# Three products taken through a LayerNorm on the unnormalized residual, with weights split further ahead

## The chip, the cores and the metric

The program runs on one core of one Trainium2 chip. The metric is the device time of one execution in microseconds (us). The kernel before took 2340.74 us (median of three executions, 2340.49 to 2344.26).

## The reference, cut to what matters

The model is a two-layer encoder on 256 tokens of width 1024, in fp32. In each layer two sub-layers are wrapped by a LayerNorm:

```python
h = x * (1.0 + scale1) + shift1
aq, ak, ..., gl = split(h @ w_in[l])            # 70 column blocks of 128
...                                             # four mixers, gated merge -> mix
x = layer_norm(ALPHA * x + gate1 * mix, ln_g[l, 0], ln_b[l, 0])      # "ln1"
h2 = x * (1.0 + scale2) + shift2
q = h2 @ wq ; s = q . subkeys ; top 16 per half                      # p_wq: 16 column blocks
y = sum of expert rows of u_tab, v_tab                               # u: 128 blocks, v: 128 blocks
x = layer_norm(ALPHA * x + gate2 * y, ln_g[l, 1], ln_b[l, 1])        # "ln2"
```

`layer_norm` is `(x - mean) * rsqrt(var + eps) * g + b`, over the 1024 features of each token.

## The kernel before, in words

Features lie on the partitions: a residual `r` is 8 chunks of 128 features by 256 tokens. All weights are streamed from HBM once. A product is one job: 128 output features by 256 tokens, summed over the 8 input chunks. Fp32 accuracy is reached with three fp32r passes: weight `w` and input `x` are each split in a high and a low part, and `prod` issues wlo·xhi, whi·xlo and whi·xhi for each chunk, so 24 matmuls of 128x256 (L238 to L240). The weight arrives by SyncE's DMA queue as `raw` (512 KB), ScalarE makes `whi` (L230), VectorE `wlo` = raw - whi (L233). There are three such pairs of buffers, so a product's split waits until the product three before it is done.

The jobs of one layer are, in this order: 70 w_in products with the mixers beside them, 16 w_br products (merge into `gacc`, split into `h`), 8 w_out products (each makes one chunk of `r`, L832, and its square and sums for the norm), ln1, 16 p_wq products (each with four small `ssc` matmuls, L905, and a search of the 16 largest on VectorE, `topk`, L93), 128 u and 128 v products, ln2. In front of a norm the weights of the next three products are already split ("areas": raw in `raws`, split in `areas`). Four norms are run: ln1 and ln2 of layer 0, ln1 of layer 1, and the last one, which writes the output.

A norm (`norm`) runs as follows. TensorE sums r and r² with matmuls against a vector of ones (`lnst`, L348); it repeats a product with no use (`warm`, L332) while it would wait. VectorE computes mean and rsqrt with three Newton steps on 128x2 values (L352 to L359). TensorE spreads the two rows over the partitions (`lnb`, L325). VectorE multiplies and adds (L369) chunk by chunk. Then for each chunk `emit` lets ScalarE apply the affine map g·(1+scale), b·(1+scale)+shift (L386, `hf`) and make the high part (L230, `h`), VectorE the low part (L233). The three area products take the chunks as they come. ScalarE also rescales the residual for the next norm (L396) and stores it to HBM (`xd`).

The program's text gives only the dependences. A scheduler reorders each engine's queue, within an engine everything is issued in the order of that queue, and every wait is on another engine's or a DMA's semaphore. `behind` and `InOrder` pin a few orders.

## Time and profile before

| | |
|---|---|
| median of three executions | 2340.74 us (2340.49 to 2344.26) |
| the profiled execution | 2339.15 us, of which the span is 2337.3 us |
| mean granted TensorE clock | 0.994 of full speed |
| TensorE busy | 2285.6 us of 2337.3, 98% |
| VectorE, ScalarE, GpSimd busy | 77%, 60%, 10% |
| chain of work that ended last | TensorE 88%, VectorE 5%, DMA 3%, ScalarE 2% |

TensorE (PE) is the bound nearly everywhere. A busy TensorE can still do work of no use: the `warm` matmuls count as busy. A matmul of 128x256 shows 0.28 us, but the next starts 0.12 us later; so 24 of them are 2.88 us of the engine. VectorE (DVE) instructions of 128x256 show 0.41 to 0.47 us and start 0.34 to 0.39 us apart; ScalarE (ACT) ones with a scale show 0.59 us and start 0.5 us apart.

### The profile page before, as it was taken

How to read it: one execution, taken by the hardware profiler on the slowest of the kernel's cores; microseconds unless marked ns; L12 is line 12 of the kernel's file. 1: busy time of each engine (PE TensorE's matmuls, PEld its weight loads, DVE VectorE, ACT ScalarE, POOL GpSimd, SP SyncE). 2: the span in 40 equal slices, each digit the busy share in tenths (PEclk: the TensorE clock that was granted, in tenths of full speed). 3: DMA queues.
4: the chain of work that ended last, by engine and by line, in shares of the span. 5: the costliest groups of instructions: out<-in, count | busy, mean ns of one | idle time of the engine just before them, and what ended most of it. 6: DMA issues, size and time to landing. Idle time of an engine off the chain costs nothing.

```text
span 2337.3 us, 41336 instructions
## 1 busy us (share of the span) xinstructions
PE 2285.6 (98%) x14624; PEld 2022.1 (87%) x14624; DVE 1806.1 (77%) x3867; ACT 1414.0 (60%) x3069; POOL 240.9 (10%) x282
## 2 busy tenths in 40 slices
PE   5999999999999999999999999999999999999998
PEld 4999999888888888888899999998888888888887
DVE  6778798997889677777666676889888896665555
ACT  5666645677776654545456665457777766454544
POOL 0000000222222200000000000102222222000000
PEclk9999999999999999999999999999999999999999
DMA  9666664788888988888754455548888889766663
GB/s 352 207 215 208 208 215 146 200 219 206 205 207 205 233 269 277 274 292 288 239 182 141 150 172 155 198 154 213 226 205 206 205 213 240 234 211 194 195 211 109
DMA packets 165326, 495.49 MB, mean 212 GB/s; under 512 B 19584, under 2 KB 57216, under 8 KB 161920
## 3 DMA queue, kind: packets, MB, share of 16 engines
q1 hardware_dynamic: 127248, 453.51, 61.6%
q0 software_dynamic: 36864, 33.57, 9.5%
q10 hardware_dynamic: 1008, 5.77, 0.7%
q8 instruction: 116, 1.90, 0.3%
q14 instruction: 90, 0.74, 0.1%
HBM read 450.57 MB, written 5.24 MB: 195 GB/s over the span
## 4 chain that ended last, share of the span: by engine, by line
PE 88%; DVE 5%; DMA 3%; ACT 2%; issue 1%; SPq 0%; ACTq 0%; DVEq 0%
PE main L246 18%; PE vacc L1120 10%; PE vacc L1122 10%; PE vacc L1121 10%; PE main L247 9%; PE main L238 8%; PE main L239 7%; PE main L240 7%; DVE wlo L233 1%; PE gw L1020 1%; PE gw L1021 1%; DVE topk L93 1%; DMA raw<-in_w_in 1%; PE pt L530 1%; DMA ada<-in_w_ada 1%
## 5 line engine op out<-in xcount | busy, mean ns | idle before, releaser
L233 DVE TENSOR_TENSOR wlo<-raw,whi 128x1024 fp32r<-128x1024 f32 x723 | 880.7, 1219 | 362.9 <-ACT whi L230 353.6
L230 ACT ACTIVATE whi<-raw 128x1024 fp32r<-128x1024 f32 x720 | 763.4, 1060 | 551.8 <-PE vacc L1122 304.9
L246 PE MATMUL main<-h,whi 128*128 128x512 f32 x2048 | 731.3, 400 | 0.4 <-ACT whi L230 0.4
L247 PE MATMUL main<-h,wlo 128*128 128x256 f32 x2048 | 573.6, 280 | 1.7 <-DVE wlo L233 1.7
L246 PEld LDWEIGHTS main<-h,whi 128*128 128x128 f32 x2048 | 384.4, 188 | 85.0 <-ACT whi L230 0.7
L238 PE MATMUL main<-h,wlo 128*128 128x256 f32 x1408 | 410.0, 292 | 4.3 <-DVE wlo L233 3.0
L1120 PE MATMUL vacc<-whi,wv 128*128 128x512 f32 (+1 forms) x1030 | 400.0, 389 | 2.1 <-ACT u L1076 1.9
L1121 PE MATMUL vacc<-wlo,wv 128*128 128x512 f32 (+1 forms) x1030 | 399.7, 388 | 0.0
L240 PE MATMUL main<-h,whi 128*128 128x256 f32 x1408 | 399.6, 284 | 0.0
L1122 PE MATMUL vacc<-whi,wv 128*128 128x512 f32 (+1 forms) x1030 | 399.5, 388 | 0.0
L239 PE MATMUL main<-h,whi 128*128 128x256 f32 x1408 | 398.9, 284 | 0.0
L247 PEld LDWEIGHTS main<-h,wlo 128*128 128x128 f32 x2048 | 386.3, 189 | 3.4 <-DVE wlo L233 3.0
L1077 POOL DMA_DIRECT2D u<-more x256 | 220.4, 861 | 707.4 <-ACT u L93 414.9
L238 PEld LDWEIGHTS main<-h,wlo 128*128 128x128 f32 x1408 | 270.4, 192 | 9.6 <-DVE wlo L233 4.8
L239 PEld LDWEIGHTS main<-h,whi 128*128 128x128 f32 x1408 | 270.9, 193 | 0.5
L240 PEld LDWEIGHTS main<-h,whi 128*128 128x128 f32 x1408 | 270.6, 192 | 0.1
L1120 PEld LDWEIGHTS vacc<-whi,wv 128*128 128x128 f32 x1030 | 193.2, 188 | 43.0 <-ACT u L1076 2.8
L1121 PEld LDWEIGHTS vacc<-wlo,wv 128*128 128x128 f32 x1030 | 193.3, 188 | 40.0 <-DVE wlo L233 0.5
L1122 PEld LDWEIGHTS vacc<-whi,wv 128*128 128x128 f32 x1030 | 193.3, 188 | 39.9
L309 POOL TENSOR_TENSOR lnss<-lnss,sq 128x256 f32<-128x256 f32 x22 | 20.3, 922 | 1373.3 <-ACT sq L304 1372.7
L1002 DVE TENSOR_TENSOR ohe<-iota,ijg 128x1024 f16<-128x1024 f16 x128 | 87.4, 685 | 17.4 <-PE gw L1021 17.4
L1075 ACT ACTIVATE more<-main 128x256 f32<-128x256 f32 x256 | 96.3, 376 | 4.7 <-PE main L247 4.7
(244 smaller groups left out, 2847.2 us busy)
## 6 DMA issues: line engine op xcount, KB each, us to landing
raw<-in_p_u SPq DMA_DIRECT2D x256, 512.0 KB, 4.5
raw<-in_p_v SPq DMA_DIRECT2D x256, 512.0 KB, 3.8
raw<-in_w_in SPq DMA_DIRECT2D x134, 512.0 KB, 4.0
u<-more POOLq DMA_DIRECT2D x256, 128.0 KB, 5.2
adav<-in_w_ada SPq DMA_DIRECT2D x56, 512.0 KB, 5.5
raw<-in_w_br SPq DMA_DIRECT2D x32, 512.0 KB, 3.6
raw<-in_p_wq SPq DMA_DIRECT2D x26, 512.0 KB, 3.5
mixA<-in_w_ada SPq DMA_DIRECT2D x24, 512.0 KB, 4.7
```

The costliest lines, as they stand in the source:

```text
L230: return S.activation(hi, src, AF.Copy, scale=scale)
L233: return V.tensor_tensor(lo, src, hi.bitcast(F32), op=OP.subtract)
L238: PE.matmul(out, wlo(c), x(c)[:, 0], start=c == 0, stop=False)
L239: PE.matmul(out, whi(c), x(c)[:, 1], start=False, stop=False)
L240: PE.matmul(out, whi(c), x(c)[:, 0], start=False, stop=c == n - 1)
L246: PE.matmul(out, whi(c), x(c), start=c == 0, stop=c == n - 1, skip_group_check=True)
L247: PE.matmul(out[:, 0], wlo(c), x(c)[:, 0], start=False, stop=c == n - 1, skip_group_check=True)
L1075: S.activation(more, out[:, 1], AF.Copy)
L1077: nc.gpsimd.dma_start(u, more, accum_op=OP.add)
L1120: PE.matmul(o, wl[:, tt], hi, start=first, stop=False, skip_group_check=o0 > 0)
L1121: PE.matmul(o, wh[:, tt], lo, start=False, stop=False, skip_group_check=o0 > 0)
L1122: PE.matmul(o, wh[:, tt], hi, start=False, stop=last, skip_group_check=o0 > 0)
```

## The change

At three of the four norms (all but the last) the first three products ("heads") no longer wait for the normalized input. They take `xr` = g·(1+scale)·r, split in high and low, which `early_chunk` makes for each chunk as soon as its residual is there (ScalarE L296, VectorE L297), with two more columns that carry the affine terms (128x258 instead of 128x256). The result is copied out of PSUM (`ho`, ScalarE L403), and when mean and rsqrt are known, `head` normalizes it: one ScalarE instruction (`hu`, L358), a VectorE multiply (L359) and add (L360). The 13 remaining p_wq products, or 67 w_in products, still take the normalized `h`. The warm matmuls are left at the last norm only, without the 14 behind `lnb`.

At ln1 the raw area weights go to a free slice of `state["m"]`, and are allocated, loaded and split ahead of the first w_out product. The w_out jobs are marked `over`: weights are split so far ahead that the products 4, 5 and 6 of p_wq are split during w_out. At ln2 of layer 0 six w_in weights rather than three are loaded and split in the v phase (`NHEAD`), and the w_ada loads there are spread over 4.5 rather than 5 jobs each.

```diff
+    def new_early(x, sc, sh, g, b):
...
+        V.tensor_tensor(fold[:, 0, 0], g, opsc, op=OP.mult)
...
+        S.activation(x[:, :, 0, T:], ss, AF.Copy)
+        V.tensor_tensor(x[:, :, 1, T:], ss, x[:, :, 0, T:].bitcast(F32), op=OP.subtract)
+
+    def early_chunk(r, m):
+
+        x, sc = state["xr"][:, m], fold[:, 0, 0, m:m + 1]
+        S.activation(x[:, 0, :T], r, AF.Identity, scale=sc)
+        V.scalar_tensor_tensor(x[:, 1, :T], r, sc, x[:, 0, :T].bitcast(F32), op0=OP.mult, op1=OP.subtract)
...
+    def head(j, o, b):
+
+        u = wk.tile([128, T], F32, name="hu", tag="t1k", bufs=6)
+        S.activation(u, b[1], AF.Identity, scale=o[:, T:T + 1], bias=o[:, T + 1:])
+        V.tensor_tensor(o[:, :T], o[:, :T], b[0], op=OP.mult)
+        V.tensor_tensor(o[:, :T], o[:, :T], u, op=OP.add)
+        j.mm = lambda hi, lo: o[:, :T]
+
+    def norm(r, emit, heads=(), banks=()):
...
-        warm(early)
+        if not heads:
+            warm(6)
...
-        warm(22)
+        if not heads:
+            warm(22)
...
-        if state["ready"] is not state.get("last_hi"):
-            warm(14)
+        todo = []
+        for j, k in zip(heads, banks):
+            out = bank(k, [128, XW], name="head")
+            prod(out, lambda c: j.split[0][:, c], lambda c: j.split[1][:, c], lambda c: state["xr"][:, c], NC8)
+            o = wk.tile([128, XW], F32, name="ho", tag="more", bufs=4)
+            S.activation(o, out, AF.Copy)
+            todo.append(lambda j=j, o=o: head(j, o, b))
         for m0, m1 in ((0, 1), (1, 2), (2, 4), (4, 6), (6, 8)):
...
             for m in range(m0, m1):
                 emit(m)
+            if m0 and todo:
+                todo.pop(0)()
...
+        def out_areas():
+            state["areas"] = big.tile([128, NAREA, 2, NC8, 128], F32R, name="areas", tag="gB0")
+            state["raws"] = state["m"][:, 13:13 + NAREA * D // T].rearrange("p a b -> p (a b)")
+            new_early(big.tile([128, NC8 * 2 * XW], F32R, name="xr", tag="gB1"), mods[l][:, 32:40], mods[l][:, 24:32], pv(P_LNG + 16 * l, 8), pv(P_LNB + 16 * l, 8))
...
         def out_begin():
-            new_areas("gB1")
...
                 stats(r, m, 1, V.scalar_tensor_tensor(r, out, mods[l][:, 16 + m:17 + m], r, op0=OP.mult, op1=OP.add))
+                early_chunk(r, m)
...
+        jobs.append(Job(func=out_areas))
         for m in range(NC8):
             outs.append(out_job(m))
+            outs[-1].over = True
...
+            if l + 1 < DEPTH:
+                e = big.tile([128, NHEAD * 2 * D + NC8 * 2 * XW], F32R, name="early", tag="gA")
...
-                n = (10 if len(todo) < 12 else 5) * i + 2 * k
+                n = (20 if len(todo) < 12 else 9) * i // 2 + 2 * k
...
-            lows = split_his(k + 1 + LOOK)
+            n = k + 1 + LOOK
+            if j.over:
+                while sum(not x.area for x in srcs[k + 1:n]) < LOOK:
+                    n += 1
+            lows = split_his(n)
```

The lines of the changed kernel that make a weight split are L232 (ScalarE) and L235 (VectorE); the residual's rescaling is L429, the affine map L419, the w_out residual L869, the merge L826 and L829. Three places of the engines' queues follow, all at ln1 of layer 0.

The first is the start of the w_out products. `gacc` is the last merged chunk, from which `h` is split for all w_out products; `mixA` with `main` is a residual chunk. On VectorE before:

```order
L791 TENSOR_TENSOR gm_3996<-gm_3996,mixA_241 128x512
L233 TENSOR_TENSOR wlo_4004<-raw_3893,whi_4003 128x1024
L793 TENSOR_TENSOR gacc_3999<-gm_3996 128x256
L796 SCALAR_TENSOR_TENSOR h_3399<-gacc_3999,h_3399 128x256
L832 SCALAR_TENSOR_TENSOR mixA_241<-main5_4009,mods0_78,mixA_241 128x256
L832 SCALAR_TENSOR_TENSOR mixA_241<-main0_4048,mods0_78,mixA_241 128x256
L307 TENSOR_TENSOR lnss0_4035<-mixA_241 128x256
L233 TENSOR_TENSOR wlo_4043<-raw_3931,whi_4042 128x1024
```

and in the changed kernel:

```order
L291 TENSOR_TENSOR xr_4004<-fold_92,xr_4004 128x8x2
L235 TENSOR_TENSOR areas_4003<-mixA_241,areas_4003 128x1024
L826 TENSOR_TENSOR gacc_3999<-gm_3996 128x256
L235 TENSOR_TENSOR areas_4003<-mixA_241,areas_4003 128x1024
L829 SCALAR_TENSOR_TENSOR h_3399<-gacc_3999,h_3399 128x256
L235 TENSOR_TENSOR areas_4003<-mixA_241,areas_4003 128x1024
L869 SCALAR_TENSOR_TENSOR mixA_241<-main5_4019,mods0_78,mixA_241 128x256
L869 SCALAR_TENSOR_TENSOR mixA_241<-main0_4058,mods0_78,mixA_241 128x256
L235 TENSOR_TENSOR wlo_4053<-raw_3931,whi_4052 128x1024
```

The three low splits of the areas have moved from between the w_out weights to around the merge of the last chunk. On TensorE, in the changed kernel, at the border between the third (`main1_4099`) and the fourth w_out product (`main5_4137`):

```order
L240 MATMUL main1_4099<-h_3399,wlo_4014 128x256
L241 MATMUL main1_4099<-h_3399,whi_4013 128x256
L242 MATMUL main1_4099<-h_3399,whi_4013 128x256
L240 MATMUL head2_4367<-xr_4004,areas_4003 128x258
L240 MATMUL main5_4137<-h_3399,wlo_4053 128x256
L241 MATMUL main5_4137<-h_3399,whi_4052 128x256
```

One matmul of the third head has moved in ahead of the fourth product; before, that product followed the third directly.

The second place is ScalarE behind `lnb`, where the chunks of `h` are made. Before:

```order
L230 ACTIVATE h_4289<-hf_4384 128x256
L396 ACTIVATE mixA_241<-mixA_241,fold_92 128x256
L386 ACTIVATE hf_4390<-mixA_241,fold_92 128x256
L386 ACTIVATE hf_4394<-mixA_241,fold_92 128x256
L230 ACTIVATE h_4289<-hf_4390 128x256
L230 ACTIVATE h_4289<-hf_4394 128x256
L386 ACTIVATE hf_4400<-mixA_241,fold_92 128x256
L386 ACTIVATE hf_4404<-mixA_241,fold_92 128x256
L230 ACTIVATE h_4289<-hf_4400 128x256
L230 ACTIVATE h_4289<-hf_4404 128x256
```

and in the changed kernel:

```order
L419 ACTIVATE hf_4466<-mixA_241,fold_92 128x256
L419 ACTIVATE hf_4470<-mixA_241,fold_92 128x256
L232 ACTIVATE h_4325<-hf_4466 128x256
L232 ACTIVATE h_4325<-hf_4470 128x256
L358 ACTIVATE hu_4474<-lnb7_4362,ho_4419 128x256
L429 ACTIVATE mixA_241<-mixA_241,fold_92 128x256 x2
L419 ACTIVATE hf_4480<-mixA_241,fold_92 128x256
L419 ACTIVATE hf_4484<-mixA_241,fold_92 128x256
L232 ACTIVATE h_4325<-hf_4480 128x256
L232 ACTIVATE h_4325<-hf_4484 128x256
L358 ACTIVATE hu_4488<-lnb7_4362,ho_4446 128x256
L429 ACTIVATE mixA_241<-mixA_241,fold_92 128x256 x2
```

For each pair of chunks one `hu` (L358) and two rescalings (L429) now stand between; of the eight rescalings six stood behind the last chunk before.

The third place is VectorE behind the last chunk of `h`. `topk` is the search on one product's scores; of the weights split there, `wlo_4485`, `wlo_4522` and `wlo_4569` belong to products 5, 6 and 7 of p_wq before, `wlo_4566` to product 7 after. Before:

```order
L233 TENSOR_TENSOR wlo_4485<-raw_4159,whi_4484 128x1024
L93 MAX topk_4428<-topk_4428 128x8 x2
L93 MATCH_REPLACE topk_4428<-topk_4428 128x128 x2
L93 MAX topk_4428<-topk_4428 128x8 x2
L93 MAX_INDEX topk_4428<-topk_4428 128x8 x4
L233 TENSOR_TENSOR wlo_4522<-raw_4197,whi_4521 128x1024
L93 MAX topk_4428<-topk_4428 128x8 x2
L93 MATCH_REPLACE topk_4428<-topk_4428 128x128 x2
L93 MAX topk_4428<-topk_4428 128x8 x2
L93 MAX_INDEX topk_4428<-topk_4428 128x8 x4
L233 TENSOR_TENSOR wlo_4569<-raw_4300,whi_4568 128x1024
```

and in the changed kernel:

```order
L283 TENSOR_SCALAR fold_92<-prm_75 128x8
L284 TENSOR_SCALAR fold_92<-prm_75 128x8
L95 MAX topk_4512<-topk_4512 128x8 x2
L95 MATCH_REPLACE topk_4512<-topk_4512 128x128 x2
L95 MAX topk_4512<-topk_4512 128x8 x2
L95 MAX_INDEX topk_4512<-topk_4512 128x8 x4
L95 MAX topk_4512<-topk_4512 128x8 x2
L95 MATCH_REPLACE topk_4512<-topk_4512 128x128 x2
L95 MAX topk_4512<-topk_4512 128x8 x2
L95 MAX_INDEX topk_4512<-topk_4512 128x8 x4
L235 TENSOR_TENSOR wlo_4566<-raw_4255,whi_4565 128x1024
```

The splits of products 5 and 6 have moved away, to the w_out stage; between the last chunk and the split of product 7 there are now the searches of two products and nothing else.

## Rows read from the trace of the kernel before

**Rows 1.** The page: the chain that ended last, by engine.

```profile
PE 88%; DVE 5%; DMA 3%; ACT 2%; issue 1%; SPq 0%; ACTq 0%; DVEq 0%
```

**Rows 2.** TensorE's timeline, ln1 of layer 0 (start us, duration us, instruction).

```profile
360.87 0.95 PE L348 MATMUL lnst<-ones,lnss 128*128 128x1 f32 x8
...
362.59 2.88 PE L332 MATMUL warm<-areas 128*128 128x256 f32 x22
365.57 0.69 PE L325 MATMUL lnb<-ident,rs 128*128 128x128 f32 x4
...
367.99 0.62 PE L238 MATMUL main<-h,areas 128*128 128x256 f32 x3
...
388.70 0.36 PE L238 MATMUL main<-h,wlo 128*128 128x256 f32 x1
```

**Rows 3.** ScalarE's timeline, w_out and ln1 of layer 0.

```profile
343.48 1.06 ACT L230 ACTIVATE whi<-raw 128x1024 fp32r<-128x1024 f32 x1 [1.14 <-PE main L240]
...
344.75 0.40 ACT L304 ACTIVATE sq<-mixA 128x256 f32<-128x256 f32 x1
...
367.34 0.60 ACT L386 ACTIVATE h<-mixA,fold 128x256 fp32r<-128x256 f32 x1 [5.27 <-DVE mixA L369]
...
371.72 1.08 ACT L386 ACTIVATE hf<-mixA,fold 128x256 f32<-128x256 f32 x2
...
373.32 1.08 ACT L386 ACTIVATE hf<-mixA,fold 128x256 f32<-128x256 f32 x2
...
374.92 3.05 ACT L396 ACTIVATE mixA<-mixA,fold 128x256 f32<-128x256 f32 x6
377.87 0.36 ACT L1052 ACTIVATE qf<-main 128x256 f32<-128x256 f32 x1
```

**Rows 4.** VectorE's timeline, w_out, ln1 and p_wq of layer 0.

```profile
341.48 0.42 DVE L793 TENSOR_TENSOR gacc<-gm 128x256 f32<-128x256 f32 x1
342.38 0.42 DVE L796 SCALAR_TENSOR_TENSOR h<-gacc,h 128x256 fp32r<-128x256 f32 x1 [0.48 <-ACT h L230]
...
344.69 1.22 DVE L233 TENSOR_TENSOR wlo<-raw,whi 128x1024 fp32r<-128x1024 f32 x1
...
374.74 0.76 DVE L233 TENSOR_TENSOR h<-hf,h 128x256 fp32r<-128x256 f32 x2 [0.84 <-ACT h L230]
...
380.88 0.48 DVE L93 MAX8 topk<-topk 128x8 f32<-128x128 f32 x2
...
383.23 1.21 DVE L233 TENSOR_TENSOR wlo<-raw,whi 128x1024 fp32r<-128x1024 f32 x1
```

**Rows 5.** TensorE's timeline, ln2 of layer 0 and the first w_in products of layer 1.

```profile
1182.10 0.60 PE L325 MATMUL lnb<-ident,rs 128*128 128x128 f32 x4
...
1194.59 0.39 PE L238 MATMUL main<-h,wlo 128*128 128x256 f32 x1
...
1206.92 0.38 PE L238 MATMUL main<-h,wlo 128*128 128x256 f32 x1 [0.56 <-DVE wlo L233]
```

**Rows 6.** VectorE's timeline, ln2 of layer 0: the last chunks of h.

```profile
1191.09 0.75 DVE L233 TENSOR_TENSOR h<-hf,h 128x256 fp32r<-128x256 f32 x2
```

**Rows 7.** A v-phase stretch: busy of PE, PEld, DVE, ACT, POOL; PEclk, DMA, GB/s.

```profile
1060.00:1160.00 100.00, 100.00 (x443) 82.81 (x442) 75.34 (x105) 50.52 (x74) 0.00 (x0) 1.00 0.81 275
```

**Rows 8.** TensorE's idle times longer than the usual, by its timeline.

```profile
30.68 0.38 PE L238 MATMUL main<-h,areas 128*128 128x256 f32 x1 [1.61 <-DVE opsc L417]
...
484.64 0.38 PE L247 MATMUL main<-h,wlo 128*128 128x256 f32 x1 [0.76 <-DVE wlo L233]
...
516.91 0.23 PE L1020 MATMUL gw<-ohe,oha 128*128 128x128 f16 x1 [1.27 <-DVE oha L1005]
...
1506.92 0.39 PE L238 MATMUL main<-h,wlo 128*128 128x256 f32 x1 [0.42 <-DVE wlo L233]
```

**Rows 9.** TensorE alone by stretches: busy, count, granted clock (PEclk), DMA.

```profile
31.00:35.00 4.00, 4.00 (x23) 0.57 1.01 395
517.00:519.00 2.00, 1.60 (x14) 1.00 0.78 208
```

More of the change, by code (lines that the diff above doesn't have):

```diff
@@ L27 @@
 NAREA = 3
+NHEAD = 6
+XW = T + 2
 NCAND = 4 * 16 + 12 * 4
@@ L98, in __init__ @@
         self.src, self.mm, self.post, self.func, self.pre = src, mm, post, func, pre
-        self.ready, self.hooks, self.area, self.split = False, [], False, None
+        self.ready, self.hooks, self.area, self.split, self.over = False, [], False, None, False
 def hybrid_encoder(tc, A, stop=None, dump=None):
@@ L329, in warm @@
         out = bank(2, [128, T], name="warm")
-        a = state["ready"]
+        a = state["last_hi"]
         for i in range(n):
             tc.keep_in_program_order(PE.matmul(out, a[:, 0], a[:, 0:2].rearrange("p c m -> p (c m)"), start=True, stop=True))
-    def norm(r, emit, ready, early=0):
-        state["ready"] = ready
+    def head(j, o, b):
[5 more added lines that the diff above has]
+    def norm(r, emit, heads=(), banks=()):
         with behind(state["stats_end"]):
-            lows = split_his(nsplit + 1 + sum(j.area for j in srcs[nsplit:nsplit + NAREA]))
+            n = nsplit
+            while n < len(srcs) and srcs[n].area:
+                n += 1
+            lows = split_his(n + 1)
             half = NC8 // 2
@@ L393, in emit @@
             marks["lo"] = split_lo(x[:, m, 1], h, x[:, m, 0])
-        norm(r, emit, state['areas'][:, 0, 0], early)
+        norm(r, emit, heads, banks)
         for m in range(NC8):
@@ L1200, in ln2 @@
                 state["h"] = new_h()
-                norm_to_h(r, state["h"], mods[l + 1][:, 8:16], mods[l + 1][:, 0:8], g, b, 6)
+                norm_to_h(r, state["h"], begin_areas[l + 1][:NAREA], (1, 2, 3))
             else:
@@ L1205, in emit @@
                     nc.sync.dma_start(A["out"][:, m], r[:, m])
-                norm(r, emit, state['last_hi'], 6)
+                norm(r, emit)
         jobs.append(Job(func=ln2))
@@ L1218, in _body @@
         j.area = True
-    areas_of(begin_areas[1], state["vjobs"], 121)
+    for i, j in enumerate(begin_areas[1][:NHEAD]):
+        j.area = True
+        state["vjobs"][112 if i < NAREA else 109 + 2 * i].hooks.append(lambda i=i, j=j: area_load(i, j))
+        state["vjobs"][114 + 2 * i].hooks.append(lambda i=i, j=j: area_split(i, j))
     if stop is not None:
```

34 lines of the change are left out of this document (21 added, 13 removed).

## The prediction, made before the changed kernel was run

> **What bounds the kernel now.** I read the chain of waits first: TensorE holds 88% of what ended last [rows 1], so time can only come from stretches in which TensorE waits or does work of no use. Then TensorE's timeline at the norms. At ln1 of layer 0 the sums begin at 360.87, `lnb` stands at 365.57, and the first useful matmul at 367.99 [rows 2]: 7.1 us, filled with sums and warm matmuls. The area products follow at the pace of the chunks of `h`, whose last pair of low parts starts at 374.74 [rows 4]. With the waits for chunks, p_wq product 7 starts at 388.70 [rows 2]. I use that start as the mark at which to compare: by then six products are done in either kernel. The timelines of ScalarE and VectorE then tell what would be late once TensorE has other work. At ln2 of layer 0 the marks are `lnb` at 1182.10, the fourth product at 1194.59, and a stall of 0.56 at 1206.92 [rows 5]. With 2.88 us for a product, product 9 begins at 1194.59 + 5 x 2.88 + 0.56 = 1209.55.
>
> **The change, part by part.**
>
> *Work added.* The heads' matmuls are 258 columns rather than 256: under 1% of three products of 2.88, at most 0.1 us a norm. Each residual chunk costs ScalarE one `xr` high part, nearest row L386 with 0.60 us, half a microsecond apart [rows 3], and VectorE one low part, nearest L796 with 0.42 [rows 4]. Such pairs could cost nothing, if they fit into ScalarE's waits (1.14 us ahead of 343.48 [rows 3]), up to 8 x 0.6 = 5 us if TensorE waited for each. I take nothing for the chunks after the first, since a w_out product leaves ScalarE 2.88 us for a weight split of 1.06, a square of 0.40 and this 0.6 [rows 3], and price the first one by itself.
>
> *Start of w_out (ln1, both layers).* The three area splits now stand around the last merged chunk on both engines. Before, `gacc` began at 341.48 and the last `h` low part at 342.38, 0.42 long, so done at 342.80 [rows 4]. One low split of 1.22 us and a bit [rows 4] lies ahead of `gacc`, another between it and the low part: worked through the two queues, `gacc` comes 1.6 later and `h` is done at 344.95. TensorE has the early parts of three w_out products to do meanwhile, and is through the third at about 346.35. Next in its queue is one matmul of the third head, which needs `xr` of residual chunk 0. That chunk's product is finished about 345.3; ScalarE then has two weight splits, a square and `xr` in its queue, 2 x 1.0 + 0.3 + 0.6 apart: 348.3. The `wlo` of the fourth product comes about 348.05. So TensorE idles from 346.35 to 348.4, **+2.05 us**. With the split ahead of the merge hidden in waits it would be 0; with a full third split in the way, 3.2.
>
> *The norm itself.* w_out ends 2.1 later, at 362.97. Twelve head matmuls (1.5 us) lie among the sums in TensorE's queue and one `xr` low part (0.35) in VectorE's chain, so `lnb` comes at 369.6 instead of 365.57. The warm matmuls go, which frees nothing: TensorE now has the heads there, 8.6 us of useful work.
>
> *The chain of h.* Before, a pair of chunks took ScalarE 1.6 us (371.72 to 373.32), and six of the eight rescalings stood behind the last pair (374.92, 3.05 us for six) [rows 3]. Now a pair has one `hu` and two rescalings between, 0.5 each: 3.1 us. The first chunk starts at 371.75 (before 367.34 [rows 3]) because two head results are copied ahead of it, and the last low part is done at 383.6 (before about 375.5). For `hu`, which reads PSUM, the nearest rows are 0.36 for `qf` from PSUM and 0.60 for L386 [rows 3]; I take the 0.5 between starts, and 0.2 less for each of three would be 0.6 us in all. Six products are then through at 385.5, some 2.8 us ahead of before.
>
> *Product 7.* Its low split stands on VectorE behind the searches of the first two products. A search with nothing ahead of it takes 383.23 - 380.88 = 2.35 us [rows 4]. The first search needs `qf` of head 1, which stands behind the whole chain of `h` on ScalarE (before it stood at 377.87 [rows 3], behind the six rescalings): the search starts about 385.8. Two searches end at 390.5, the split of 1.2 at 391.65, and product 7 starts at 391.7 instead of 388.70: **+3.0 us** for ln1 of layer 0, the 2.05 included. In layer 1 the queues are the same, and the stall of 0.42 at 1506.92 [rows 8], where w_out waited for a split, goes: **+2.6**.
>
> *ln2 of layer 0.* Here the fillers cost time: behind the warm matmuls `lnb` stood at 1182.10 [rows 5]. Now `lnb` comes at about 1183.25, since head matmuls lie among the sums, and the chain of `h` at 3.1 us a pair ends at 1196.3; before, the last pair's low parts began at 1191.09 [rows 6]. But six weights are split beforehand and no search is in the way: six products are through at 1197.9, product 7 starts at 1199.15 when a bank has been copied out, product 9 at 1199.15 + 2 x 2.88 = 1204.9, **-4.65** against 1209.55. The three extra loads and splits in the v phase cost nothing as long as its reserve holds: TensorE is busy 100 of 100 us there, DVE 75.3, ACT 50.5, DMA 0.81 [rows 7]. Without it, three low splits of 1.22 would show, 3.7 us.
>
> *Given back.* In layer 0 TensorE waits later for VectorE: 0.76 at 484.64 and 1.27 at 516.91 [rows 8]. VectorE has less to do after product 7 than before (two weight splits of 1.2 gone, three multiplies and adds of heads come), so part of the 3.0 can disappear there. From nothing to all 2.03; I take half, **-1.0**.
>
> *The clock.* After the idle 1.61 us ahead of 30.68 [rows 8] TensorE ran 31 to 35 at a mean granted clock of 0.57, thus mostly at the 1.2 GHz level [rows 9]: 4 x 0.43 = 1.7 us lost. After 1.27 idle, 517 to 519 was granted 1.00 [rows 8, 9], the 2.4 GHz level. The two new waits at each ln1 (2.05 us, and some 6 us between product 6 and product 7 broken only by small `ssc` matmuls) are both longer than the first of these: from nothing to 4 x 1.7 = 6.8. I take one of four, **+1.7**, since the second pair falls in time that VectorE's searches set anyway, and the first in a stage where later waits absorb some of it.
>
> The Trainium skill, "TensorE: Matmul & The Clock Gate", section "What's actually happening", says the throttled state is the default and activity releases it. By that rule every one of the four waits would count, and removing the warm matmuls speaks against this change; the sum would be 5.1 higher. The two rows above agree with it only in part: one idle was followed by the low level, one was not.
>
> **Sum.** +3.0 + 2.6 - 4.65 - 1.0 + 1.7 = +1.65, on the profiled execution's 2339.15: 2340.8. The median of the runs shown is 1.6 above that execution, so I set the time at 2342.4.
>
> The Trainium skill, "Perfetto Trace Analysis", section "Tensor Engine Instruction", holds that TensorE's queue can only bring a weight load forward past matmuls under way, while the others are strictly in order. By it the single head matmul does hold up the fourth product; if matmuls could pass it, 0.3 us of the 2.05 would go, as `wlo` is late as well. The 1.61 us ahead of 30.68 [rows 8] agree with it.
>
> **Rivals.**
>
> *Faster: the two ln1s do not lose.* If the area splits fit into the waits at the merge, the 2.05 is gone in both layers, and if the search of product 1 is not held behind the whole chain of `h`, or the pairs take 2.6 rather than 3.1, another 1 to 2 us each. For it: ScalarE waited 1.14 us ahead of 343.48 and 5.27 ahead of 367.34 [rows 3]. Against it: the queues as they stand, in which `qf` is behind the last pair. 0.95 + 0.55 - 4.65 - 2.0 (all given back) = -5.2, up to -9: 2335.5 down to 2331.7.
>
> *Slower: the clock falls in each of the four waits and nothing is given back.* Mechanism: the fillers kept TensorE active up to the first product; now it has true idle of 2 us in front of the fourth w_out product and a stretch of mere `ssc` in front of product 7. For it: the rows of 31 to 35 [rows 9]. Against: 517 to 519. Price 0.95 + 6.8 = +7.7: 2348.5. It decides from three drops of the four on (0.95 + 5.1 = 6).
>
> *The change does not do what it says:* the heads run, but ln2 gains nothing because the chain of `h` ends 4.5 us later than before and the splits of products 7 to 9 or the store of the residual come late. Then +1.65 + 4.65 = +6.3: 2347.0.
>
> **How the numbers follow.** A difference under 0.2% (4.7 us) cannot be told from none here. The forecast has 0.42, with its own range 2337 to 2345.4; the faster rival 0.28, the clock 0.22, no gain at ln2 0.08. So faster 0.28, same 0.42, slower 0.30. To leave out at most 2 in 10 the range reaches to 2332.5 on the one side and 2349.5 on the other.
>
> **What would show it.** In TensorE's timeline: an idle of about 2 us in front of the fourth w_out product, named as waiting for ScalarE's `xr` or VectorE's `wlo`; `lnb` 6.6 us behind the end of w_out rather than 4.7; a wait of 4 to 6 us for VectorE's `wlo` in front of p_wq product 7, with two searches just ahead of that split; product 9 of layer 1's w_in 21.7 us behind the norm's `lnb` rather than 27.5. PEclk in slices right behind both waits shows the clock. The forecast is wrong if product 7 follows product 6 without a wait, if the area splits leave no idle at w_out, or if the u phase takes back nothing or more than 2 us.

## The result and the profile after

The changed kernel took 2357.53 us (median of 4 runs, 2356.2 to 2358.81) beside 2342.5 for the kernel before on the same chip: ratio 1.0064, interval 1.0047 to 1.0082. It is slower by 15 us, 17 against the 2340.8 that all executions of the kernel before in this study give, and it lies above the predicted range. I had given slower 0.30.

The profiled execution of after has 2357.85 us and a span of 2356.0, 18.7 more than before. Its page, chain by engine:

```profile
PE 83%; DVE 8%; DMA 4%; ACT 3%; issue 2%; SPq 0%; POOL 0%; ACTq 0%; DVEq 0%; POOLq 0%
```

TensorE falls from 88% [rows 1] to 83; VectorE, the transfers and ScalarE gain. So the added time is waiting, and time at a lower clock. Where it arises, by marks on TensorE in the two profiled executions (lost at low clock: the sum of 1 minus the granted clock over pieces of 1 us around the norm):

| stretch of TensorE's timeline | before | after | change | lost at low clock, before / after |
|---|---|---|---|---|
| ln1, layer 0: start to last `ssc` | 424.64 | 430.81 | +6.2 | 0 / 5.1 |
| u phase and v phase, to the last v matmul | 746.02 | 745.25 | -0.8 | |
| ln2: last v matmul to first `pt` of layer 1 | 62.64 | 66.77 | +4.1 | 3.4 / 5.1 |
| ln1, layer 1: first `pt` to last `ssc` | 340.39 | 348.19 | +7.8 | 0 / 5.1 |
| the rest | 763.6 | 765.0 | +1.4 | |

The first stretch holds a gain of 1.9 that is not the change's (layer 0's first attention scores stand at 75.34 instead of 77.19): behind the wait at 30.7, which both kernels have (1.61 before [rows 8], 1.59 after), before ran at 0.57 [rows 9] and after at 1.00. Without it ln1 of layer 0 lost 8.1. The profiled execution of after is also the one of its four that lost the most clock (23.6 us in all, the others 16.5 to 21.2).

TensorE's timeline of after at ln1 of layer 0 (start, duration, instruction, idle before it and what ended it):

```profile
346.13 0.39 PE L240 MATMUL head<-xr,areas 128*128 128x258 f32 x1 [1.77 <-ACT xr L296]
...
360.88 0.61 PE L380 MATMUL lnst<-ones,lnss 128*128 128x1 f32 x4
362.60 0.76 PE L380 MATMUL lnst<-ones,lnss 128*128 128x1 f32 x4 [1.11 <-POOL lnss L330]
...
368.07 0.42 PE L240 MATMUL head<-xr,areas 128*128 128x258 f32 x1
...
371.68 0.60 PE L346 MATMUL lnb<-ident,rs 128*128 128x128 f32 x4
...
389.78 0.71 PE L944 MATMUL ssc<-subk,qf 128*128 128x128 f32 x4 [1.08 <-ACT topk L946]
...
393.91 0.58 PE L240 MATMUL main<-h,wlo 128*128 128x256 f32 x1 [0.43 <-DVE wlo L235]
```

Against [rows 2]: the idle at w_out is there (1.77, named as `xr`), `lnb` comes 6.1 later, and product 7 starts at 393.91 instead of 388.70. Between lie two things that I had not written down: a wait of 1.11 for a partial sum from GpSimd, and a rate. The head matmul at 368.07 takes 0.42 where others take 0.28, and its neighbours stand 0.215 apart rather than 0.12. TensorE alone by stretches (length, busy and count, granted clock, DMA share, GB/s) says why:

```profile
31.00:35.00 4.00, 3.24 (x26) 1.00 1.01 398
335.00:360.00 25.00, 23.23 (x192) 1.00 0.63 205
365.00:370.00 5.00, 5.00 (x25) 0.53 0.01 3
370.00:375.00 5.00, 5.00 (x45) 1.00 0.33 105
394.00:396.00 2.00, 2.00 (x9) 0.50 0.45 109
1185.00:1193.00 8.00, 8.00 (x44) 0.57 0.09 12
```

The idle of 1.77 did not lower the clock (335 to 360 is 1.00). It fell to the 1.2 GHz level at the sums, whose matmuls have one column, and after the short `ssc` matmuls ahead of product 7. Between 365 and 370, 25 matmuls run where 45 do in the next 5 us. The last line is ln2.

ScalarE, then VectorE, in the chain of `h` of after:

```profile
380.45 1.09 ACT L419 ACTIVATE hf<-mixA,fold 128x256 f32<-128x256 f32 x2
381.45 0.71 ACT L232 ACTIVATE h<-hf 128x256 fp32r<-128x256 f32 x2
382.06 0.55 ACT L358 ACTIVATE hu<-lnb,ho 128x256 f32<-128x256 f32 x1
382.51 1.08 ACT L429 ACTIVATE mixA<-mixA,fold 128x256 f32<-128x256 f32 x2
383.69 1.09 ACT L419 ACTIVATE hf<-mixA,fold 128x256 f32<-128x256 f32 x2
...
386.29 0.40 ACT L1091 ACTIVATE qf<-ho 128x256 f32<-128x256 f32 x1
```

```profile
381.88 0.76 DVE L235 TENSOR_TENSOR h<-hf,h 128x256 fp32r<-128x256 f32 x2 [1.47 <-ACT h L232]
...
382.98 0.68 DVE L407 TENSOR_TENSOR mixA<-mixA,lnb 128x512 f32<-128x512 f32 x1
385.12 0.76 DVE L235 TENSOR_TENSOR h<-hf,h 128x256 fp32r<-128x256 f32 x2 [1.47 <-ACT h L232]
...
387.97 0.49 DVE L95 MAX8 topk<-topk 128x8 f32<-128x128 f32 x2 [1.31 <-ACT topk L946]
...
392.66 1.20 DVE L235 TENSOR_TENSOR wlo<-raw,whi 128x1024 fp32r<-128x1024 f32 x1
```

A pair of chunks now takes 3.24 (383.69 - 380.45) against 1.60 in [rows 3], `qf` comes 8.4 later than there, and the split of product 7 stands behind two searches, as forecast. To be seen as well: VectorE's add at L407 for a pair stands *behind* the low parts of the pair before, and each engine is fed by the other in turn.

ln2 of layer 0: TensorE of before from the last v matmul to the first sum, then TensorE and VectorE of after, beside [rows 5]:

```profile
1170.66 0.28 PE L1122 MATMUL vacc<-whi,wv 128*128 128x256 f32 x1
...
1173.56 0.61 PE L348 MATMUL lnst<-ones,r 128*128 128x1 f32 x4 [0.72 <-DVE r L1196]
```

```profile
1176.06 0.29 PE L1162 MATMUL vacc<-whi,wv 128*128 128x256 f32 x1
...
1182.97 0.50 PE L380 MATMUL lnst<-ones,r 128*128 128x1 f32 x4
...
1192.66 0.60 PE L346 MATMUL lnb<-ident,rs 128*128 128x128 f32 x4
...
1209.60 0.39 PE L240 MATMUL main<-h,wlo 128*128 128x256 f32 x1 [1.39 <-ACT mixA L745]
...
1219.92 0.39 PE L240 MATMUL main<-h,wlo 128*128 128x256 f32 x1 [1.42 <-DVE wlo L235]
...
1233.82 0.38 PE L240 MATMUL main<-h,wlo 128*128 128x256 f32 x1 [1.91 <-DVE wlo L235]
...
1235.15 1.13 PE L580 MATMUL s<-mixA 64*128 64x256 f32 x8 [0.82 <-DVE mixA L517]
```

```profile
1175.27 0.96 DVE L328 TENSOR_TENSOR lnss<-r 128x256 f32<-128x256 f32 x1
1176.15 0.96 DVE L297 SCALAR_TENSOR_TENSOR early<-r,fold,early 128x256 fp32r<-128x256 f32 x1
1177.04 0.41 DVE L328 TENSOR_TENSOR lnss<-lnss,r 128x256 f32<-128x256 f32 x1
1177.37 0.47 DVE L297 SCALAR_TENSOR_TENSOR early<-r,fold,early 128x256 fp32r<-128x256 f32 x1
1177.77 0.86 DVE L1242 SCALAR_TENSOR_TENSOR r<-vt,gq,r 128x256 f32<-128x256 f32 x2
...
1217.51 0.43 DVE L95 TENSOR_TENSOR mixA<-mixA,mixG 128x256 f32<-128x256 f32 x1 [5.21 <-DMA ropet<-mixA]
...
1218.65 1.22 DVE L235 TENSOR_TENSOR wlo<-raw,whi 128x1024 fp32r<-128x1024 f32 x1
```

From the last v matmul (1176.06) to the first sum it takes 6.9 us and to `lnb` 16.6, before (1170.66) 2.9 and 11.4; from `lnb` to product 9 it takes 22.7 (1209.60 + 2 x 2.88 - 1192.66), before 27.45. So the six split products do save 4.75, and three more waits, 4.15 us in all, give most of it back before `pt`: `lnb` to `pt` is 50.2 against 51.2. The first of these waits is made on VectorE: it idles 5.21 us for the rope copies (`ropet`), and the split `wlo` that TensorE waits for at 1219.92 stands behind the rope operations in its queue.

### The profile page after: what moved, and what is told of

Same layout as the page of the kernel before. It is cut to its first block, busy times and chain, and to the rows that moved or that the text cites. A ratio compares the mean times of both kernels' runs of the same rounds, so it can differ in the third digit from the quotient of the medians.

```text
span 2356.0 us, 41206 instructions
## 1 busy us (share of the span) xinstructions
PE 2283.8 (97%) x14510; PEld 2017.1 (86%) x14510; DVE 1826.0 (78%) x3912; ACT 1431.1 (61%) x3114; POOL 244.5 (10%) x282
## 3 DMA queue, kind: packets, MB, share of 16 engines
q10 hardware_dynamic: 1008, 5.77, 0.7%
## 4 chain that ended last, share of the span: by engine, by line
PE 83%; DVE 8%; DMA 4%; ACT 3%; issue 2%; SPq 0%; POOL 0%; ACTq 0%; DVEq 0%; POOLq 0%
PE main L248 16%; PE vacc L1160 10%; PE vacc L1161 10%; PE vacc L1162 10%; PE main L249 8%; PE main L240 7%; PE main L241 7%; PE main L242 7%; DVE topk L95 3%; DVE wlo L235 2%; PE gw L1059 1%; PE gw L1060 1%; DMA raw<-in_p_u 1%; PE pt L563 1%; DMA ada<-in_w_ada 1%
## 5 line engine op out<-in xcount | busy, mean ns | idle before, releaser
L235 DVE TENSOR_TENSOR wlo<-raw,whi 128x1024 fp32r<-128x1024 f32 x720 | 876.5, 1218 | 343.1 <-ACT whi L232 337.4
L232 ACT ACTIVATE whi<-raw 128x1024 fp32r<-128x1024 f32 x717 | 760.1, 1060 | 536.1 <-PE vacc L1162 277.4
L241 PE MATMUL main<-h,whi 128*128 128x256 f32 x1384 | 393.4, 285 | 0.0
L242 PE MATMUL main<-h,whi 128*128 128x256 f32 x1384 | 393.0, 285 | 0.0
```

The source lines that it names most:

```text
L232: return S.activation(hi, src, AF.Copy, scale=scale)
L235: return V.tensor_tensor(lo, src, hi.bitcast(F32), op=OP.subtract)
L241: PE.matmul(out, whi(c), x(c)[:, 1], start=False, stop=False)
L242: PE.matmul(out, whi(c), x(c)[:, 0], start=False, stop=c == n - 1)
```

## The experiments

All ratios are to the kernel before, on the same chip. Two figures come beside each median where they matter: "lost" is the span times (1 minus the mean granted clock), averaged over the executions, and "rest" is the median less that. Before: lost 12.6, rest 2328.2. After: lost 20.0, rest 2337.5. Counted one for one, 7.4 of the 16.7 us are clock and 9.3 are waits or work. The clock's part is more likely smaller: among executions of one kernel, one that lost 1 us more took 0.64 us longer on average (after and the 18 kernels below, 118 executions; 0.70 in 79 executions of before). The clock is given to three decimals, steps of 2.3 us, which blurs this somewhat.

### The sums, the rescalings and the clock

**e1_sums_first.** All head matmuls are put behind the last sum.

```diff
+            with behind(end):          # end: the last lnst matmul
                 prod(out, lambda c: j.split[0][:, c], lambda c: j.split[1][:, c], lambda c: state["xr"][:, c], NC8)
```

> The heads' matmuls are ordered behind the last matmul of the sums (lnst) at all three norms; nothing else differs from the changed kernel. Theory A (the sums lie among head matmuls and the stretch runs at the low clock, so lnb comes 10.8 us behind the end of w_out): lnb comes about 7.5 us behind it, 3 us earlier at each norm, and 2348 to 2350 us in all. Theory B (the chain of h on ScalarE and the searches on VectorE decide, whatever lnb does): TensorE only waits longer further on, 2356 to 2359 us, as the changed kernel's 2357.5.

2365.44, ratio 1.0094 (1.0078 to 1.0111), lost 28.4, rest 2337.1. Neither theory; the rest is that of after, and what came on top is clock. TensorE in it:

```profile
348.96 0.39 PE L240 MATMUL main<-h,wlo 128*128 128x256 f32 x1 [1.38 <-DVE wlo L235]
...
366.35 1.00 PE L380 MATMUL lnst<-ones,lnss 128*128 128x1 f32 x4 [1.11 <-POOL lnss L330]
...
374.15 0.60 PE L346 MATMUL lnb<-ident,rs 128*128 128x128 f32 x4
```

The sums now run with nothing between them, and more time is spent at the low clock. VectorE has the last input of `lnb` ready 7.8 us behind the first sum instead of 10.2, but `lnb` then stands 1.7 us in the queue behind head matmuls at the low clock (0.6 in after). The matmuls among the sums were of use. At w_out, where no head matmul stands in the way now, 1.38 of the 1.77 us of idle remain, for `wlo`.

**e2_rescale_late.** The rescalings at L429 and the store of the residual are put behind the last high part of `h`.

```diff
+        with behind(marks["hi"]):
             for m in range(NC8):
                 S.activation(r[:, m], r[:, m], AF.Identity, scale=fold[:, 1, 0, m:m + 1], bias=fold[:, 1, 1, m:m + 1])
             S.dma_start(xd, r)
```

> The eight rescalings of the residual are ordered behind the last high part of h at all three norms. Theory B: a pair of chunks takes ScalarE 2.1 us rather than 3.24, so the last low part of h is done 3.3 us earlier; at ln2 product 7 starts 3 us earlier; at the two ln1s the first qf then stands behind eight rescalings, not two, so the first search starts no earlier and product 7 gains nothing (within 1 us). In all 2353.5 to 2355.5 us. Theory A: what decides lies ahead of lnb, and nothing changes: 2356 to 2359 us.

2364.40, ratio 1.0100 (1.0083 to 1.0117). The pairs stayed at 3.24 us (TensorE takes them up at 376.32, 379.56, 382.81) although two rescalings of 0.54 had left each of them, and eight rescalings then stood ahead of `qf`. This breaks the step that a pair takes 3.1 us because of the amount of ScalarE's work alone.

**e4_sums_rescale.** Both edits.

> Both edits of the two kernels above: heads behind the sums, rescalings behind the chain of h. Theories A and B together: 3 us a norm from the sums and 3 us at ln2 from the chain, 2344 to 2347 us; if either alone is the bound, no better than the better of the two.

2374.36, ratio 1.0145 (1.0128 to 1.0162), lost 38.0, rest 2336.4: both misses add, and what they add is clock.

**e3_direct2.** TensorE sums the last two residual chunks itself at ln1, so that it needn't wait for GpSimd's partial sum.

```diff
-                stats(r, m, 1, V.scalar_tensor_tensor(r, out, mods[l][:, 16 + m:17 + m], r, op0=OP.mult, op1=OP.add))
+                stats(r, m, 2, V.scalar_tensor_tensor(r, out, mods[l][:, 16 + m:17 + m], r, op0=OP.mult, op1=OP.add))
```

> At the two ln1s TensorE sums the last two residual chunks itself, instead of one, so the last addition on GpSimd is one w_out product earlier; 4 more sum matmuls. Theory C (the 1.11 us that TensorE waits for GpSimd in front of the sums is what the low clock follows, 362.7 to 369.7): the wait goes and the clock stays at its upper level, lnb 1.1 + 3 us earlier at each ln1, 2349 to 2351 us. Theory A without it: only the 1.1 us goes at each ln1, the stretch stays at the low clock, 2355 us. Theory B: 2356 to 2359 us.

2355.57, ratio 1.0060 (1.0043 to 1.0076), lost 18.8. The wait of 1.11 is gone; the median is 2 lower, which the noise covers. In the profiled execution the clock fell elsewhere, at 349 to 352, behind the same idle of 1.77 that left it up in after. (Of the profiles with this idle in layer 0, the clock stayed up behind it in after, e2, e5, e6, e9 and e13 and fell in e3, e8, e11, e14 and e15.) Its ln2, which the edit doesn't touch, ran from the last v matmul (1177.46) to `lnb` at full clock:

```profile
1185.00:1193.00 8.00, 7.04 (x59) 1.00 0.00 0
```

```profile
1191.30 0.62 PE L346 MATMUL lnb<-ident,rs 128*128 128x128 f32 x4
```

`lnb` comes 13.8 us behind the last v matmul there, 16.6 in after; but `pt` comes 66.5 behind it, 66.8 in after.

**e5_fill_sums.** Twelve useless matmuls on area weights ahead of the sums at ln1.

```diff
+        elif banks[0] == 2:
+            warm(12, 6, state["areas"][:, 0, 0])
```

> At the two ln1s 12 matmuls without use (128x256, on the area weights) stand between the last w_out product and the sums, where the changed kernel idled 1.11 us for GpSimd; in the queue the sums then also come ahead of the heads' matmuls. Theory C (the low level behind the sums follows from TensorE having too little to do there): the granted clock stays at the upper level from the sums to lnb, lnb about 6.5 us behind the end of w_out rather than 10.8, and product 7 is 3 us earlier at each ln1: 2351 to 2353 us. Rival B (chain of h and searches): lnb earlier, product 7 not: 2356 to 2359 us. If the order of sums and heads is what hurts (as with the heads behind the sums, 2365 us), 2360 us or more.

2357.98, ratio 1.0078 (1.0061 to 1.0095), lost 20.0. The sums of layer 0 ran at full clock, those of layer 1 did not, and in total nothing was won. So these fillers are no remedy; no run put the 22 fillers behind the sums back beside the heads.

**e6_split7** and **e11_pool_split7.** Product 7's split goes ahead of the second search; in e11 with the rescalings on GpSimd (below).

```diff
+        if j.first:                    # the first six p_wq products
+            split_los(lows)
         over = bgs["topk"].run(1.6 - over)
-        split_los(lows)
```

> In the first six p_wq products the low splits of the weights come ahead of the searches in the program, so on VectorE one search rather than two stands in front of the split of product 7; nothing else. Theory D (product 7 waits for its split behind the searches): product 7 starts 2.3 us earlier at both ln1s, and the stretch of small ssc matmuls in front of it is shorter: 2352 to 2354 us. Rival: the searches are the bound anyway up to the u phase, and the 2.3 us come back as waits at 484 to 524 us: 2356 to 2359 us.

> Rescalings on GpSimd, and in p_wq one search rather than two ahead of the low split of product 7. Theories F and D together: another 2 us at each ln1 less than with the rescalings alone, 2341 to 2346 us. If the searches are the bound up to the u phase (theory D wrong): as with the rescalings alone.

2359.41 (1.0084; 1.0063 to 1.0106) and 2356.75 (1.0068; 1.0050 to 1.0087), no gain over after or e9. Product 7 starts at 391.31 in e6 instead of 393.91, and a later product waits: 0.43 at 400.59 in e6, 2.22 at 399.18 in e11. The searches have to be done in any case: an order in VectorE's queue doesn't shorten them.

### ln1 and ln2 apart

**e7_ln1_old.** ln1 is put back: areas split at the start of w_out, warm matmuls, no heads there; ln2 keeps the change.

```diff
-            norm_to_h(state["r"], state["h"], wqs[:NAREA], (2, 3, 4))
+            norm_to_h(state["r"], state["h"], (), ())
```

> Both ln1s as in the kernel before (areas, warm matmuls, no heads, no further look ahead); ln2 of layer 0 with the heads and the six early weights. By the marks of the two traces ln2 alone loses 4.1 us between the last v matmul and the first attention scores of layer 1 and the ln1s 7 and 8.5: 2345 to 2347 us. If losses at one norm were paid by another (the clock, or the v phase with its larger loads), the sum would differ: 2350 us or more, or no more than before, 2342 us. My recorded step (ln2 gains 4.65): 2337 to 2338 us.

2345.98, ratio 1.0026 (1.0016 to 1.0036), lost 12.8. So the change at ln2 alone costs 5.2 (4 to 8 by the interval), and on average no more clock is lost than before. In its profile 3.3 of that lie between the last v matmul and `pt`, and 1.5 in the v phase. The forecast was -4.65. The two ln1s carry the other 11.5 by the medians, 9 by the ratios, with 7.2 more lost in clock.

**e8_rope_act** and **e10_ln1_old_rope_pool.** SyncE issues a burst of eight small copies in after at just the time of the second wait at ln2:

```profile
1209.99 7.19 SPq L510 DMA_DIRECT2D ropet<-mixA  x8
```

e8 issues the first three products' copies from ScalarE's queue, e10 (on e7) from GpSimd's.

```diff
-                    nc.sync.dma_start(rot[a:a + 32], dst[b:b + 32])
+                    (S if l == 1 and n < 3 else nc.sync).dma_start(rot[a:a + 32], dst[b:b + 32])
```

> The 12 small rope copies of the first three w_in products of layer 1 are issued from ScalarE's DMA queue rather than SyncE's, where in the changed kernel 8 of them in a row (7.2 us) stood ahead of the next weights; nothing else. Theory E (behind ln2 the heads finish together, and their copies hold up the weights): the waits of 1.42 and 1.91 us at 1219.9 and 1233.8 go, 2354 to 2355.5 us. Rival (those waits are from VectorE's queue, where the rope products stand ahead of the low splits, or cost ScalarE as much as they free): 2356.5 to 2359 us.

> Heads at ln2 alone (2346 us), with the 12 small rope copies of the first three w_in products of layer 1 issued from GpSimd's DMA queue, where nothing waits behind them. Theory E (a burst of copies holds up the queue that it is in: 7.2 us on SyncE, 10.4 on ScalarE, where TensorE waited 7.0): with an idle queue the waits of 1.2 and 2.0 us behind ln2 go, 2342.5 to 2344 us. Rival (the weights are late for another reason, as the bandwidth that the 1 MB bias loads take): 2345.5 to 2347 us.

e8: 2362.12 (1.0102; 1.0085 to 1.0119). ScalarE, then TensorE in it:

```profile
1206.00 10.39 ACTq L510 DMA_DIRECT2D ropet<-mixA  x8
1216.44 1.06 ACT L232 ACTIVATE whi<-raw 128x1024 fp32r<-128x1024 f32 x1 [10.19 <-DMA ropet<-mixA]
```

```profile
1218.80 0.58 PE L240 MATMUL main<-h,wlo 128*128 128x256 f32 x1 [7.04 <-DVE wlo L235]
```

The burst holds the queue that issues it, and on ScalarE a weight split stood behind it. e10: 2345.76 (1.0021; 1.0010 to 1.0033), equal to e7. That the burst is issued on SyncE is not what costs ln2 its gain. But VectorE waits for what the copies bring in either case, 5.21 us in after and 6.75 in e10, with a weight split behind it. That is the rival named for e8; it is read from the traces, and no run put the split ahead of the rope operations.

### The chain of h

**e9_pool_rescale.** The eight rescalings and the store run on GpSimd. **e12_before_pool** does the same in the kernel before.

```diff
-            S.activation(r[:, m], r[:, m], AF.Identity, scale=fold[:, 1, 0, m:m + 1], bias=fold[:, 1, 1, m:m + 1])
-        S.dma_start(xd, r)
+            nc.gpsimd.tensor_scalar(r[:, m], r[:, m], fold[:, 1, 0, m:m + 1], fold[:, 1, 1, m:m + 1], op0=OP.mult, op1=OP.add)
+        nc.gpsimd.dma_start(xd, r)
```

> The eight rescalings of the residual, and its store, move from ScalarE to GpSimd at all three norms; else the changed kernel. Theory F (behind lnb ScalarE is the bound: 13 us of affine maps, high parts, rescalings and the heads' own instructions, whatever the order; ordering the rescalings last only moved the wait to the first qf): pairs take 2.1 us, the first qf follows the last pair at once, product 7 starts 4 us earlier at each ln1 and 3 to 4 at ln2: 2345 to 2349 us. Rival (GpSimd's additions slow VectorE, or the searches and the clock decide): 2354 us or more.

> The kernel before, with only the rescalings and the store on GpSimd. Theory F: there ScalarE had 10.6 us of work behind lnb against 8.64 us of products, with two rescalings (1.0 us) ahead of chunk 2: the three products end 1 us earlier at each of three norms, 2336.5 to 2339.5 us. Rival (TensorE's order and VectorE set that stretch): as before, within 1 us.

e9: 2356.26 (1.0049; 1.0025 to 1.0073); e12: 2341.0 (1.0001; 0.9991 to 1.0011). ScalarE in e9:

```profile
382.89 1.09 ACT L419 ACTIVATE hf<-mixA,fold 128x256 f32<-128x256 f32 x2 [1.21 <-DVE mixA L407]
...
386.25 1.09 ACT L419 ACTIVATE hf<-mixA,fold 128x256 f32<-128x256 f32 x2 [1.21 <-DVE mixA L407]
```

Without a rescaling in its queue ScalarE idles 1.21 a pair, and the pair still takes 3.36. There is a second limit as long as the first, a round trip: ScalarE's affine maps, and with them the high parts, wait for VectorE's add at L407, which stands behind the low parts of the pair before, which wait for ScalarE's high parts.

**e13_lead** takes that round trip away and leaves the rescalings on ScalarE; **e14_lead_pool** takes both.

```diff
+        apply(*groups[0])                        # multiply and add, L407
+        for g, (m0, m1) in enumerate(groups):
+            if g + 1 < len(groups):
+                apply(*groups[g + 1])            # the next pair's, ahead
             for m in range(m0, m1):
                 emit(m)                          # this pair's parts of h
```

> The multiply and add of the next pair of chunks come ahead of this pair's low parts on VectorE, at every norm; else the changed kernel. Theory G (a round trip between ScalarE and VectorE sets the 3.24 us of a pair): pairs come 2.1 us apart, the last low part 3.3 us earlier; at the ln1s six rescalings then stand ahead of the first qf, so product 7 gains about 1 us, at ln2 2 to 3 us: 2352 to 2355 us. Theory F (amount of ScalarE work): pairs 3.1 us or the rescalings simply move, 2356 to 2358 us.

> The same lead on VectorE, and the rescalings and the store on GpSimd. Theory G: pairs 2.1 us apart and the first qf at once behind them, product 7 some 4 us earlier at each ln1, 3 us at ln2: 2345 to 2349 us. If the round trip is not it: 2355 us or more, as with the rescalings on GpSimd alone (2356 us).

ScalarE in e13, then in e14:

```profile
376.17 1.09 ACT L425 ACTIVATE hf<-mixA,fold 128x256 f32<-128x256 f32 x2
...
378.21 1.10 ACT L425 ACTIVATE hf<-mixA,fold 128x256 f32<-128x256 f32 x2
...
381.86 3.07 ACT L435 ACTIVATE mixA<-mixA,fold 128x256 f32<-128x256 f32 x6
384.82 0.41 ACT L1097 ACTIVATE qf<-ho 128x256 f32<-128x256 f32 x1
```

```profile
376.52 1.09 ACT L425 ACTIVATE hf<-mixA,fold 128x256 f32<-128x256 f32 x2
...
381.27 1.08 ACT L425 ACTIVATE hf<-mixA,fold 128x256 f32<-128x256 f32 x2
...
382.87 1.02 ACT L1097 ACTIVATE qf<-ho 128x256 f32<-128x256 f32 x3
```

e13: 2357.3 (1.0079; 1.0055 to 1.0104), lost 23.6, rest 2333.7. The pairs are 2.05 apart, but six rescalings then stand ahead of `qf`. e14: 2343.99 (1.0018; 1.0006 to 1.0029), lost 16.9, rest 2327.1; the two pairs between its first two rows take 2.05 and 2.70. The four medians (ratios): neither 2357.5 (1.0064), rescalings 2356.3 (1.0049), round trip 2357.3 (1.0079), both 2344.0 (1.0018). Neither alone is clear of the noise of four or five executions, the two together give 11 to 13.5. In the rests (2337.5, 2338.4, 2333.7, 2327.1) the round trip alone takes off 3.8, which its clock gives back. This shows two limits side by side. In e14's profile product 7 starts at 390.61, and ln2 from the last v matmul to `pt` takes 60.1 us: 2.6 less than before, where after took 4.1 more. The profile of e12, before with the rescalings moved alone, has 60.5 there, so against it little is left. What is left of e14's loss against the kernel before is the lost clock, 16.9 against 12.6.

**e15_lead_pool_split7_direct2** adds e6 and e3 to e14.

> As e14, with one search rather than two ahead of product 7's split and the last two chunks summed by TensorE at the ln1s. Theories D and G: another 2 us at each ln1 and 1 us at the sums: 2339 to 2344 us. If the searches are the bound up to the u phase: as e14.

2344.34 (1.0016; 1.0006 to 1.0027): nothing more; a wait of 2.22 comes at 397.17.

**e16_ln2_best** keeps ln1 as before, and has e14's chain and GpSimd's copies at ln2.

> Heads at ln2 alone, with the lead on VectorE and the rescalings on GpSimd at all norms and the first rope copies in GpSimd's queue. Theory G at ln2: 3 us less than with heads at ln2 alone (2346 us), and the low parts no later at the ln1s: 2341 to 2343.5 us. If what is left at ln2 is the burst of copies (now behind GpSimd's rescalings), 2345 us or more.

2343.28 (1.0011; 1.0002 to 1.0021), lost 12.2. In its profile ln2 takes 60.2, 2.4 less than before, yet the time isn't lower: 2.8 come ahead of the sums of layer 0, where no edit is, and 2.2 between the last `ssc` of layer 1 and the u phase. In the first stretch a weight lands late (ScalarE idles 5.77 for it ahead of 60.39, TensorE 2.80 ahead of 62.76); in the second two longer waits for VectorE make 1.2 (0.76 and 1.39 against 0.51 and 0.45), and for the rest I have no reason.

**e17_pin** (on e14 with e3) and **e18_pin_only** (on after) hold the area splits until the partial sums of a w_out product, so that the idle of 1.77 goes.

```diff
+        with behind(*state.get("pin", ())):
             split_hi(j.split[0], raw)
             split_lo(j.split[1], raw, j.split[0])
```

> The kernel with the lead on VectorE and the rescalings on GpSimd (2344 us), the last two chunks summed by TensorE at the ln1s, and the low splits of the areas ordered behind a w_out product, off the last merge. Theory H (those splits make the 1.77 us idle at w_out): the idle is under 0.5 us at both layers, and the low level that followed it in some runs is gone: 2338 to 2341 us, level with or better than the kernel before. Rival (wlo of the fourth product is late by itself): idle 1.4 us or more, 2343 to 2345 us.

> The changed kernel with only the low splits of the areas moved behind a w_out product. Theory H: 1.77 us less idle at each ln1, given on to product 7: 2353 to 2355 us. Rival (what follows absorbs it): 2356 to 2359 us, with the idle gone.

2347.26 (1.0032; 1.0021 to 1.0043) and 2363.23 (1.0091; 1.0073 to 1.0109). The idle is gone in both, and splits are late elsewhere: later w_out products wait 0.46 and 0.81 in e17 and 0.80 in e18, and the sums wait. TensorE in e18:

```profile
365.44 1.05 PE L381 MATMUL lnst<-ones,lnss 128*128 128x1 f32 x8 [1.29 <-DVE lnss L329]
```

The work of VectorE and ScalarE that made the idle was only moved to where the sums wait for it. No version beat the kernel before.

## Why the prediction was wrong

**The two ln1s: right in size.** Predicted +3.0 and +2.6; by the table 8.1 - 5.1 = +3.0 and 7.8 - 5.1 = +2.7 without the clock, if each us lost is counted as a us of time. The idle at w_out was 1.77 (2.05 predicted), and product 7 had `qf` of the chain and two searches ahead of it, as worked out. The head matmul's own part of that idle, 0.3 by the forecast, is 0.4, since e1 keeps 1.38 without it. The agreement is partly luck: it rests on one pair of profiles, the wait of 1.11 for GpSimd was not in the sum, and the 3.1 us of a pair had the right length for only one of two reasons. ScalarE's amount and the round trip are equally long (3.24 with both, 3.24 and 3.36 with the round trip alone, 2.05, once 2.70, with neither between the pairs); e2, e9, e13 and e14 show it.

**The clock: mis-sized.** "I take one of four, +1.7": measured +7.4 lost on average over the executions (20.0 against 12.6), 12 at the three norms of the profiled pair; in time it is likely less. My slower rival had the amount, 6.8, but not the place. It put drops behind the idle at w_out and ahead of product 7. The second came. The first did not in after, and the larger loss lay where I had counted "8.6 us of useful work" as free: in the heads behind the sums. The step that failed is that this stretch was priced at full clock ("go, which frees nothing"): at the ln1s 3.4 of the 5.1 us were lost there. Whether the missing fillers lost it is not shown by itself: before lost as much at ln2 with its fillers in place, e3 lost nothing there without them, and 12 of them put back in e5 gave nothing. Among the rows that I had was no stretch of one-column sums without fillers behind them, and one row at 0.57 was no ground for taking one drop of four. The Trainium skill, "TensorE: Matmul & The Clock Gate", section "What's actually happening", calls the throttled state the default that activity releases. The runs bear this out in part: the three norms lose 5.1 us each in the profile of after, 0, 3.4 and 0 in that of before. They don't bear it out wait by wait, since the same idle of 1.77 was followed by 1.00 in after and by the low level in e3 and e14.

**ln2: failed.** "-4.65" came out as +4.1 in the profiled pair (1.7 of the change is clock), +5.2 by e7. Three steps make it up. Two of them failed.

First, "`lnb` comes at about 1183.25", 12.6 behind the last v matmul; it took 16.6, 4.0 more. I took "nothing for the chunks after the first" for the residual's low parts, with a reason that holds only for w_out, where a product of 2.88 lies between two chunks. At ln2 the chunks follow one another at VectorE's pace, and each L297 stands in front of the next chunk (0.47 to 0.96 us in the rows above), so the sums begin 6.9 us behind the last v matmul instead of 2.9. This is read from the traces; no run took L297 away there. The clock is the other part: in the profiles whose clock is up from there to `lnb` (e2, e3, e6, e8, e11, e15, e16, e17) `lnb` comes at 13.8, with 1.7 us lost at 15.1, with the 3.4 of after and e10 at 16.6. At full clock the low parts thus leave 1.2 above my 12.6, and the low level brings 2.8. (From the first sum to `lnb` it is 6.9 at full clock; before took 8.5 at the low one.)

Second, the step from `lnb` to product 9 held: 22.7, 21.65 predicted.

Third, I had put nothing behind product 9. There most of the 4.75 that it had gained went into the waits at 1219.92, 1233.82 and 1235.15. By e3 it is this step that decides: there `lnb` comes 2.8 earlier and `pt` only 0.3. With the chain of `h` mended (e14) `lnb` to `pt` falls from 50.2 to 45.0, 6 less than before, about what I had predicted for it, though e12 reaches 49.1 without heads.

**Given back: nothing.** The wait at the u phase fell from 1.27 [rows 8] to 0.69, but the stretch from the last `ssc` to it is 92.3 us in both kernels.

**The sum again:** 3.0 + 2.6 + 5.2 + 7.4 = 18.2, against 15 to 17 measured; the clock's 7.4 is likely too much. Of the rivals, "the clock" and "no gain at ln2" both happened, the second by the late sums and the waits behind product 9 beside the long chain of `h` that I had named. I had priced them as alternatives of 2348.5 and 2347.0, but they can happen together: 1.65 + 6.05 + 4.65 = 12.35 above the profiled time, 2353 as a median, and so far at least the range should have reached.

**Open:** why the clock falls behind one idle of 1.77 and not behind another; why VectorE's operations take 0.96 in some places of ln2 and 0.41 or 0.47 in others (GpSimd works beside it there, but no run separates this); where the last 1.0 of the 2.2 of e16 in layer 1 comes from; what the 22 fillers behind the sums would give beside the heads; whether the three more weights in the v phase, costed at nothing, cost something (it takes 351.3 us before, 350.6 in after, 352.8 in e7, 354.8 in e14).

## What to carry to other kernels

When useful work replaces fillers ahead of a chain, price three things apart: the clock, which can be low where the fillers stood, the queue in which the work's own preparation stands, and the period of the chain behind it. Where two engines feed each other through in-order queues, compute that period both as the busier engine's amount and as the round trip; if they are equally long, experiments that remove one of them show little, and only the pair tells. Rivals that can happen together are added for the range, not set side by side.

## What the runs showed of the hardware

- At a granted clock of 0.53, 25 matmuls ran in 5 us, at 1.00 45: 0.42 us instead of 0.28 each, 0.215 apart instead of 0.12. Two such stretches a norm, of some 7 and 3.5 us, lost 5.1 us in the profile of after.
- An execution that lost 1 us more of clock took 0.64 to 0.70 us longer on average (118 executions of the changed kernels, 79 of before).
- The level after a wait is not fixed by the wait: 0.57 and 1.00 behind 1.61 and 1.59 us at the same instruction in the profiles of before and after, and behind 1.77 us the clock stayed up in six profiles and fell in five.
- Eight small copies issued in a row held SyncE's queue for 7.2 us and ScalarE's for 10.4, and the next activation waited 10.19 for them.
